# A feed-forward's second chunk: its last two blocks go up by seven products, the biases reach x by DMA, and the last chunk is reordered

## The chip, the cores and the metric

One Trainium2 chip, one of its cores. The metric is the device time of one execution in microseconds (us); of several runs the median is given. A core has five engines that matter here, each with its own queue, worked off in order: TensorE (PE; its weight loads are shown as PEld), VectorE (DVE), ScalarE (ACT), GpSimd (POOL, here almost only a queue that issues DMAs) and SyncE (SP, which issues the loads of weights).

## The reference, cut to what matters

Two layers run over 512 frames of width 1024. Each layer has two feed-forwards (hidden width 2816), and around every part stands a normalisation:

```
def swiglu_ffn(x, w_gu, w_d):
    g, u = jnp.split(x @ w_gu, 2, axis=-1)
    return (jax.nn.silu(g) * u) @ w_d

for i in range(DEPTH):                                    # DEPTH = 2
    x = layer_norm(DN_ALPHA * x + 0.5 * swiglu_ffn(x, ffn1_wgu[i], ffn1_wd[i]), ...)
    mix = mlstm_mixer(x, ...) if i == 0 else gmlp_mixer(x, ...)
    x = layer_norm(DN_ALPHA * x + mix, ...)
    x = layer_norm(DN_ALPHA * x + 0.5 * swiglu_ffn(x, ffn2_wgu[i], ffn2_wd[i]), ...)
    x = layer_norm(DN_ALPHA * x + sigmoid(x @ ple_wg[i] + ple_bg[i]) * (p[i] @ ple_wp[i]), ...)
```

So there are four feed-forwards. `layer_norm` ends with a gain and a bias over the width. The arithmetic is float32.

## The kernel before

**Numbers in two parts.** TensorE reads a rounded form of float32. So every operand is held as a high part (`whi`, `fhi`, `xh`) and a low part, the rest (`wlo`, `flo`, `xl`), and each product is three matmuls (`mm3`, lines 388 to 390): high by high, high by low, low by high. ACT makes a weight's high part by a copy (L275). The low part is either a subtraction on DVE (L284 at once; L290 when it was put off) or, for some weights, a second ACT pass that writes the negative of the high part (L281), onto which a DMA that POOL issues adds the source (L282).

**A feed-forward** (`ffn`) runs over the 2816 hidden columns in chunks of 2, 4, 4, 4, 4 and 4 blocks of 128 (`FFN_CHUNKS`). While a chunk goes up (x times the gate and up weights), the chunk before it goes down in seven products of a Strassen-like scheme (`Group`, PSUM tiles `gps`). Each down product needs a form of the hidden activations (`form`: `fhi`, `flo`) and a form of the down weights (`forms`, tiles `wquarter`), and its result is added to the residual x in SBUF (`xt`) by two DVE instructions (`residual`, L761 or L763).

- In chunks 0 and 1 (`c < UP_FROM`) the way up is plain: one tile of gate columns, then one of up columns, 24 matmuls of 512 columns each (`sup`, `fps`). After an even tile ACT takes the sigmoid-weighted gate, after an odd one DVE multiplies it in (L1192), and a down product follows.
- From chunk 2 on, two blocks go up together by seven products instead of eight (`up_products`, `UpPair`, PSUM tiles `ups`), each of 24 matmuls of 256 columns. Here s counts the products of a chunk; s modulo 7 is the product's kind r. After every odd s a down product follows. The weights come as four quarters of 512 KB (tiles `wbox`); the forms for r = 2 and r = 4 are made in place by two DVE instructions each (`up_forms`, functions `s2`, L140 and L141, and `s3`, L148 and L149). `UP_BY_DMA` and `UP_BY_DMA_2` list the kinds whose low part goes by DMA, in a chunk's first and second pair.
- The seven products need sums and differences of quarters of x (`UpForms`: t1 to t4). They are made in ten steps, one after a tile, while chunks 0 and 1 go up; the rest of t3 and t4 follows in the first products of chunk 2.

**The normalisation's gain and bias** of three feed-forwards' inputs (all but the first) are put off: x itself gets them later (`Norm.finish`, L755 and L756, one DVE instruction each for a quarter of the frames, tile `gb`), from `run_affine` at the end of chunk 0 and in chunk 1.

**The order** of the instructions is the order in which the code issues them; each engine works off its own part of it and waits at semaphores. `Weights.fill` runs ahead: whenever a product gives its weight tile back (four `main` tiles, two for the down weights), it splits the next weights in one fixed list (`W.order`), the loads of which SP issues as buffers come free.

Of the kernel before, what the change touches and what calls it, by code (L numbers as in the profile page):

```python
# [11 lines left out]
F32R = mybir.dt.float32r  # L12
AF = mybir.ActivationFunctionType
OP = mybir.AluOpType
# [3 lines left out]
P = 128  # L18
# [26 lines left out]
PLE_EXTRA = 3  # L45
UP_BY_DMA = (1, 3, 4, 5, 6)
UP_BY_DMA_2 = (1, 3, 5, 6)


class Weights:  # L50
# [4 lines left out]
    def __init__(self, nc, raw_pool, split_pool):  # L55
        self.nc = nc
        self.pools, self.free = {"main": split_pool}, {"main": W_BUFS, "none": 0}
        self.raw_pools, self.raw_bufs = {"raw": raw_pool}, {"raw": RAW_BUFS}
        self.raw_free, self.raw_at, self.raw_tags = deque(range(RAW_BUFS)), {}, {}
        self.loads, self.left, self.raws = [], [], {}  # L60
        self.queues, self.held_raws = defaultdict(deque), defaultdict(deque)
        self.order, self.next_split, self.in_place, self.by_dma = [], 0, set(), set()
        self.ready, self.taken, self.held = deque(), deque(), []
        self.apart, self.pending, self.made, self.after, self.formed = False, deque(), {}, {}, set()
        self.boxes, self.rank, self.loaded_at, self.clock = [], {}, {}, 0

    def open(self, kind, pool, n):
        self.pools[kind], self.free[kind] = pool, n
# [177 lines left out]

    def fill(self, most=1000, low=None, meanwhile=None):

        while most and self.next_split < len(self.order):
# [108 lines left out]
def hybrid_trunk(ctx: ExitStack, tc, x, p, ln_g, ln_b, ffn1_wgu, ffn1_wd, ffn2_wgu, ffn2_wd,  # L358
# [110 lines left out]

    FFN_CHUNKS = [2, 4, 4, 4, 4, 4]  # L470
    LAST = len(FFN_CHUNKS) - 1
    UP_FROM = 2
    turn_p = []

    def ffn_weights(wgu, wd, name, ple=False):
        starts = [sum(FFN_CHUNKS[:c]) for c in range(LAST + 1)]

        def forms(c):
            m = FFN_CHUNKS[c] // 2

            def quarter(i, j):
                k = starts[c] + m * i
                return kp(wd)[:, k:k + m, j * 512:(j + 1) * 512]
            loads = [W.add_load(quarter(i, j), n, name) for i, j, n in ((0, 0, 2), (0, 1, 1), (1, 1, 1), (1, 0, 2))]
            return W.forms("rows", *((j, slice(None)) for j in loads))

        first = len(W.order)
        for at in range(starts[UP_FROM]):
            if at == 0 or at == starts[UP_FROM] - 1:
                W.add(*((kp(wgu)[:, :, c0:c0 + P], [slice(None)]) for c0 in (at * P, HID + at * P)))  # L490
            elif at % 2:
                add_pairs(wgu, at * P, HID + at * P)
        tiles = W.order[first:]
        del W.order[first:]
        for c, n in enumerate(FFN_CHUNKS):
            down_w = deque(forms(c - 1) if c else ())
            if c >= UP_FROM:
                products = []
                for b in range(starts[c], starts[c] + n, 2):
                    products += W.up_forms(*(W.add_load(kp(wgu)[:, k:k + 4, c0:c0 + 2 * P], 1, "box")  # L500
                                             for c0 in (b * P, HID + b * P) for k in (0, 4)),
                                            by_dma=UP_BY_DMA if b == starts[c] else UP_BY_DMA_2)
                for s, product in enumerate(products):
                    W.order.append(product)
                    if s % 2:
                        W.order.append(down_w.popleft())
                continue
            for i in range(2 * n):
                W.order.append(tiles[2 * starts[c] + i])
                if down_w:  # L510
                    W.order.append(down_w.popleft())
        if ple:
            W.add_hook("rows", lambda hi, lo: turn_p.pop()(hi, lo))
        add_rows(wd, starts[LAST], 4, ["rowsx", "rows", "main", "main"] if ple else ["main", "rows", "rowsx", "rows"])


    ML_SLOTS = (2, 3, 4, 5, 6, 7, 11)
# [191 lines left out]
    class Norm:  # L709
# [41 lines left out]
            self.prepare(t)  # L751
            self.scale(t)

        def finish(self, t):
            vec.tensor_mul(xt[:, t], xt[:, t], self.g_bc)  # L755
            vec.tensor_add(xt[:, t], xt[:, t], self.b_bc)  # L756

    def residual(t, half, ps, first):
        dst = xt[:, t, half * 512:(half + 1) * 512]
# [9 lines left out]
        if hooks:  # L769
            hooks.pop(0)()  # L770

    def run_affine(n=1):
        for _ in range(n):
            if affine:
                affine.pop(0)()

    def set_hooks(norm):
        def turn(t, half):
            return lambda: turn_x(t, halves=(half,), norm=norm)

        def last_turn():
            turn(TB - 1, 1)()
            W.refill(4)

        hooks.extend([turn(TB - 2, 0), turn(TB - 2, 1), turn(TB - 1, 0), last_turn])
        if norm.deferred:
            affine.extend([lambda t=t: norm.finish(t) for t in range(TB)])

    def down(hs, first, norm=None, lazy=False, defer=False):

# [195 lines left out]
    class UpForms:  # L986


        def __init__(self, pool, late):
# [4 lines left out]
            both = act.tile([P, 2, 4, 256], F32R, name="t1", tag="gb")  # L994
            self.t1, self.t2, self.t4 = [both[:, 0], both[:, 1]], [], []
            self.t3 = self.quarter(0, 1)
            whole, halves = slice(0, 4), (slice(0, 2), slice(2, 4))

# [17 lines left out]
                    vec.tensor_sub(a[i], a[i], c[:, s])  # L1016

            def split_t1():
                for i, s in enumerate(halves):
# [89 lines left out]
    def ffn(layer, k, rows, late, prepare=None):  # L1109
        with stage_pool("forms", 2) as fpool, stage_pool("quarters", Q_BUFS) as qpool, \  # L1110
# [14 lines left out]

            group, hs, norm, formed = None, [], None, None

            def up_products(c, n, h):
                nonlocal norm
                for s in range(7 * n // 2):  # L1130
                    b, r = s // 7 * 2, s % 7
# [18 lines left out]
                    if s % 2:  # L1150
# [3 lines left out]
                    if s == 12 and h is not None:  # L1154
# [11 lines left out]
            for c, n in enumerate(FFN_CHUNKS):  # L1166
                if c < LAST:
                    h = hpool.tile([P, 4, SEQ], F32, name="h", tag="h")[:, :n]
                elif prepare is not None:
                    prepare()  # L1170
                if c == UP_FROM - 2:
                    formed = UpForms(tpool, late)
                W.apart = c >= UP_FROM
                if c >= UP_FROM:
                    next_group = up_products(c, n, h if c < LAST else None)
                    if c < LAST:
                        next_group.form()
                    group.add()
                    group = next_group
                for i in range(2 * n if c < UP_FROM else 0):  # L1180
                    b = i // 2
                    ps = project()
                    W.clock += 2
                    if group is not None and i:
# [3 lines left out]
                        sca.activation(sg, ps, AF.Silu)  # L1188
                        W.release()
                    else:  # L1190
                        hf = h[:, b] if c < LAST else tmp_tile("hf")
                        vec.scalar_tensor_tensor(hf, sg, 0.5, ps, op0=OP.mult, op1=OP.mult)  # L1192
                        if c == LAST:
                            hs.append(halves(W.spare(name)))
                            split(*hs[b], hf)
                        W.release()
                        run_hook()
                    if group is not None and i < 7:
                        group.product()
                        W.release(kind="rows")  # L1200
                        group.form()
                    if c == 1 and i < 3:
                        run_affine()
                    if formed is not None and (i and c == UP_FROM - 2 or i > 0 and c == UP_FROM - 1):
                        formed.step()
                    if c and i == 6:
                        next_group = Group(h, fpool)
                        next_group.form()
                if c < UP_FROM and c:
                    group = next_group  # L1210
                    group.form()
                if c == UP_FROM - 1:
                    while formed.steps:
                        formed.step()
                if c == 0:
                    group = Group(h, fpool, c == 0)
                    group.form()
                    group.form()
                if c == 0:
                    run_affine()  # L1220
            W.apart = False
            return down(hs, False, norm, lazy=layer == 0, defer=prepare is not None)

    def ffn_stage(layer, k):
# [725 lines left out]
```

## Time and profile before

| | |
|---|---|
| median of 3 runs | 2196.67 us (2195.52 to 2196.89) |
| the profiled execution, its own time | 2193.39 us |
| its span, first to last instruction | 2191.7 us |
| PE busy | 2170.3 us of the span (99%), 12821 matmuls |
| DVE busy | 1760.5 us (80%) |
| ACT busy | 1208.1 us (55%) |
| POOL busy | 226.3 us (10%) |
| mean granted TensorE clock | 0.999 |

The profiled execution is 3.3 us below the median. Busy time of matmuls is longer than their pace, since they are pipelined: one with 512 columns is shown with 0.39 us and follows the one before it by 0.23 us. So PE is judged by starts and by the idle time ahead of an instruction, not by its busy share.

### The profile page before, as it was taken

To read this page: it belongs to the slowest core of one execution; us is meant where nothing else is said; L and a number is where in the kernel's file an instruction comes from. 1 tells how busy PE (TensorE), PEld (TensorE's weight loads), DVE (VectorE), ACT (ScalarE), POOL (GpSimd) and SP (SyncE) were. 2 spreads that over 40 slices of the span, in tenths; PEclk is the share of its full clock that TensorE was granted. 3 is DMA by queue.
4 is the path that set the end of the run, shared out by engine and by line. 5 is a ranking of instruction groups with operands and counts; after the bars stand their busy time and mean duration, and the time that the engine had idled before them with its cause. 6 is when DMAs were issued, how large, how long until landed. Compare 5 with 4: busy or idle time off the path is not lost.

```text
span 2191.7 us, 32537 instructions
## 1 busy us (share of the span) xinstructions
PE 2170.3 (99%) x12821; PEld 1922.0 (88%) x12821; DVE 1760.5 (80%) x2532; ACT 1208.1 (55%) x1668; POOL 226.3 (10%) x279
## 2 busy tenths in 40 slices
PE   9999999999999999999999999999999999999998
PEld 8899997888888889999888899997888888999987
DVE  5898877786767789888887998877788679988887
ACT  4576656454546445667444566655345553666642
POOL 1011100011101101111000011110001100111100
PEclk9999999999999999999999999999999999999999
DMA  6587764366857426887531587754437743777651
GB/s 187 156 204 184 172 153 136 92 154 128 155 130 154 135 81 163 200 194 172 173 125 58 153 207 186 176 145 135 144 77 140 168 135 116 179 191 179 135 183 58
DMA packets 228097, 329.46 MB, mean 150 GB/s; under 512 B 9140, under 2 KB 163892, under 8 KB 227944
## 3 DMA queue, kind: packets, MB, share of 16 engines
q1 hardware_dynamic: 169104, 211.83, 29.8%
q0 software_dynamic: 52224, 100.86, 27.5%
q10 hardware_dynamic: 6616, 14.69, 1.9%
q8 instruction: 101, 1.65, 0.3%
q14 instruction: 52, 0.43, 0.1%
HBM read 224.58 MB, written 2.11 MB: 103 GB/s over the span
## 4 chain that ended last, share of the span: by engine, by line
PE 78%; DVE 11%; issue 4%; ACT 4%; DMA 3%; SPq 0%; POOL 0%; DVEq 0%; ACTq 0%; POOLq 0%
PE ups L390 7%; PE ups L388 7%; PE ups L389 7%; PE gps L388 6%; PE gps L389 6%; PE gps L390 6%; DMA wlo<-wbox 2%; PE dps L389 2%; PE dps L390 2%; PE dps L388 2%; DVE wlo L290 2%; PE fps L388 2%; PE fps L389 1%; PE fps L390 1%; ACT whi L275 1%
## 5 line engine op out<-in xcount | busy, mean ns | idle before, releaser
L275 ACT ACTIVATE whi<-wbox 128x1024 fp32r<-128x1024 f32 x224 | 235.7, 1054 | 242.2 <-DVE wbox L141 96.9
L390 PE MATMUL ups<-xh,wlo 128*128 128x256 f32 x1024 | 290.3, 284 | 3.2 <-DMA wlo<-wbox 3.2
L388 PE MATMUL ups<-xh,whi 128*128 128x256 f32 x1024 | 289.9, 283 | 0.0
L389 PE MATMUL ups<-xl,whi 128*128 128x256 f32 x1024 | 289.7, 283 | 0.0
L275 ACT ACTIVATE whi<-wraw 128x1024 fp32r<-128x1024 f32 (+1 forms) x212 | 217.3, 1046 | 96.7 <-DVE wraw L119 22.6
L388 PE MATMUL gps<-whi,fhi 128*128 128x512 f32 x644 | 253.0, 393 | 0.4
L389 PE MATMUL gps<-wlo,fhi 128*128 128x512 f32 x644 | 252.2, 392 | 0.0
L390 PE MATMUL gps<-whi,flo 128*128 128x512 f32 x644 | 251.4, 390 | 0.0
L282 POOL DMA_DIRECT2D wlo<-wbox x144 | 122.2, 848 | 1076.8 <-ACT wlo L281 705.0
L763 DVE TENSOR_TENSOR xt<-xt,gps 128x512 f32<-128x512 f32 x302 | 194.9, 680 | 26.7 <-PE gps L390 26.7
L284 DVE TENSOR_TENSOR wlo<-wraw,whi 128x1024 fp32r<-128x1024 f32 (+1 forms) x140 | 167.6, 1214 | 41.8 <-ACT whi L275 40.9
L390 PEld LDWEIGHTS ups<-xh,wlo 128*128 128x128 f32 x1024 | 196.2, 192 | 4.3 <-DMA wlo<-wbox 4.2
L388 PEld LDWEIGHTS ups<-xh,whi 128*128 128x128 f32 x1024 | 196.1, 192 | 3.8 <-ACT us L1085 1.6
L389 PEld LDWEIGHTS ups<-xl,whi 128*128 128x128 f32 x1024 | 196.1, 192 | 2.3
L275 ACT ACTIVATE whi<-wquarter 128x1024 fp32r<-128x1024 f32 (+1 forms) x140 | 135.3, 966 | 77.0 <-DVE wquarter L119 28.9
L281 ACT ACTIVATE wlo<-wbox 128x1024 fp32r<-128x1024 f32 x144 | 150.4, 1044 | 0.0
L390 PEld LDWEIGHTS gps<-whi,flo 128*128 128x128 f32 x644 | 120.9, 188 | 26.9
L388 PEld LDWEIGHTS gps<-whi,fhi 128*128 128x128 f32 x644 | 121.3, 188 | 23.9 <-issue 1.6
L389 PEld LDWEIGHTS gps<-wlo,fhi 128*128 128x128 f32 x644 | 121.3, 188 | 21.6
L944 DVE TENSOR_TENSOR flo<-h,fhi 128x512 fp32r<-128x512 f32 (+1 forms) x140 | 88.5, 635 | 57.6 <-ACT fhi L941 57.0
L290 DVE TENSOR_TENSOR wlo<-wquarter,whi 128x1024 fp32r<-128x1024 f32 x104 | 126.6, 1218 | 0.0
L388 PE MATMUL fps<-xh,whi 128*128 128x512 f32 x288 | 112.2, 390 | 0.0
(365 smaller groups left out, 5822.4 us busy)
## 6 DMA issues: line engine op xcount, KB each, us to landing
wlo<-wbox POOLq DMA_DIRECT2D x144, 512.0 KB, 5.8
wbox<-in_ffn_wgu_dram SPq DMA_DIRECT2D x128, 512.0 KB, 4.9
wquarter<-in_ffn_wd_dram SPq DMA_DIRECT2D x64, 512.0 KB, 5.8
wraw<-in_ml_w_in_dram SPq DMA_DIRECT2D x24, 1024.0 KB, 5.8
wlo<-wraw POOLq DMA_DIRECT2D x48, 512.0 KB, 6.4
wraw<-in_ffn_wgu_dram SPq DMA_DIRECT2D x15, 1024.0 KB, 6.0
wraw<-in_gm_w_in_dram SPq DMA_DIRECT2D x15, 1024.0 KB, 5.6
wraw<-in_ffn_wgu_dram SPq DMA_DIRECT2D x17, 512.0 KB, 4.8
```

Source lines behind the costliest of these rows:

```text
L275: self.nc.scalar.activation(hi[:, s], src[:, s], AF.Copy)
L281: self.nc.scalar.activation(lo[:, s], src[:, s], AF.Copy, scale=-1.0)
L282: self.nc.gpsimd.dma_start(lo[:, s], src[:, s], accum_op=OP.add)
L284: self.nc.vector.tensor_sub(lo[:, s], src[:, s], hi[:, s].bitcast(F32))
L290: self.nc.vector.tensor_sub(lo, src, hi.bitcast(F32))
L388: mm(ps, st[0], mv[0], start=start, stop=False, skip_group_check=more)
L389: mm(ps, st[0], mv[1], start=False, stop=False, skip_group_check=more)
L390: mm(ps, st[1], mv[0], start=False, stop=stop, skip_group_check=more)
L763: vec.tensor_add(dst, dst, ps)
L944: vec.tensor_sub(lo, src, hi.bitcast(F32))
```

## The change

- `UP_FROM` gives way to `PLAIN = 4`: the first four blocks go up plainly (chunk 0 and the first two blocks of chunk 1), and the last two blocks of chunk 1 become a pair that goes up by seven products, with the down products of chunk 0 between them. This is done in all four feed-forwards.
- The steps of `UpForms` start a chunk earlier, after the first tile, and end with chunk 1's fourth tile. t2 is made last of the first eight, and its low part now goes by ACT and a DMA of POOL, not by DVE.
- Gain and bias come at four earlier places (`AFFINE_AT`), and inside a feed-forward the bias is added by a DMA that POOL issues (line 768 after), no longer by DVE.
- In the last chunk the last down product follows s = 12 instead of s = 13 (`down_after`), the second pair's form r = 5 has its low part subtracted by DVE (`UP_BY_DMA_LAST`), and the weights of the next stage are not split before the last product up (`W.limit`).

The diff, cut to its core:

```
+UP_BY_DMA_LAST = (1, 3, 6)
...
-    UP_FROM = 2
+    PLAIN = 4
+    AFFINE_AT = ((0, 1), (0, 2), (1, 0), (1, 1))
+    def plain_blocks(c):
+        return min(FFN_CHUNKS[c], max(0, PLAIN - sum(FFN_CHUNKS[:c])))
+    def down_after(c, s):
+        return s == 12 if c == LAST and s > 11 else s % 2 == 1
...
+            plain = plain_blocks(c)
+            for i in range(2 * plain):
                 W.order.append(tiles[2 * starts[c] + i])
                 if down_w:
                     W.order.append(down_w.popleft())
+            if plain < n:
+                products = []
+                for b in range(starts[c] + plain, starts[c] + n, 2):
+                    products += W.up_forms(..., by_dma=UP_BY_DMA if b == starts[c] + plain
+                                           else UP_BY_DMA_2 if c < LAST else UP_BY_DMA_LAST)
+                for s, product in enumerate(products):
+                    W.order.append(product)
+                    if down_after(c, s):
+                        W.order.append(down_w.popleft())
...
-        def finish(self, t):
+        def finish(self, t, by_dma=False):
             vec.tensor_mul(xt[:, t], xt[:, t], self.g_bc)
-            vec.tensor_add(xt[:, t], xt[:, t], self.b_bc)
+            if by_dma:
+                pool.dma_start(xt[:, t], self.b_bc, accum_op=OP.add)
+            else:
+                vec.tensor_add(xt[:, t], xt[:, t], self.b_bc)
...
             def split_t2():
-                split(f32r(self.t2, late, "whi"), f32r(self.t2, late, "wlo"), c)
+                hi, lo = f32r(self.t2, late, "whi"), f32r(self.t2, late, "wlo")
+                sca.activation(lo, c, AF.Copy, scale=-1.0)
+                nc.gpsimd.dma_start(lo, c, accum_op=OP.add)
+                sca.activation(hi, c, AF.Copy)
             self.steps = [
                 x22, lambda: joined(b, 0, 1), t3, lambda: joined(c, 0, 0), lambda: vec.tensor_add(c, b, c),
-                split_t2, t1, split_t1]
+                t1, split_t1, split_t2]
...
-            def up_products(c, n, h):
+            def up_products(c, n, h, plain):
-                for s in range(7 * n // 2):
+                for s in range(7 * (n - plain) // 2):
...
-                    if c == UP_FROM and s in formed.last:
+                    if plain and s in formed.last:
                         formed.last[s]()
...
-                    if s % 2:
+                    if down_after(c, s):
                         group.product()
...
+                if c == LAST:
+                    W.limit = ffn_ends.pop(0)
-                for i in range(2 * n if c < UP_FROM else 0):
+                for i in range(2 * plain):
...
-                    if c == 1 and i < 3:
-                        run_affine()
+                    if (c, i) in AFFINE_AT:
+                        run_affine(by_dma=True)
-                    if formed is not None and (i and c == UP_FROM - 2 or i > 0 and c == UP_FROM - 1):
+                    for _ in range(1 if (c, i) < (1, 2) else 2):
                         formed.step()
```

What this does to the queues is shown at three places. A chunk's tiles are counted from 0, gate and up tiles alike.

**DVE, where chunk 1's fourth tile is multiplied in, in the first feed-forward of layer 1** (`h<-sg,fps` is that instruction; `xt<-xt,gps` adds a down product; `x_d` and the low part `xl<-x_f` belong to t4 and t3; the two `wbox<-wbox` make the form r = 4 of the next pair). Before, the same instruction of the chunk's eighth tile, with the pair of chunk 2 behind it:

```order
L761 SCALAR_TENSOR_TENSOR xt<-xt,gps 128x512 x2
L1192 SCALAR_TENSOR_TENSOR h<-sg,fps 128x512
L284 TENSOR_TENSOR wlo<-wquarter,whi 128x1024
L1037 TENSOR_TENSOR x_d<-x_d,x_f_11495 128x512 x2
L944 TENSOR_TENSOR flo<-h,fhi 128x512
L394 TENSOR_TENSOR xl<-x_f_11494,xh 128x4x256
L148 TENSOR_TENSOR wbox<-wbox 128x1024
L149 TENSOR_TENSOR wbox<-wbox 128x1024
```

Now, behind the fourth tile:

```order
L396 TENSOR_TENSOR t_11945<-x_a,t_11945 128x512 x2
L775 SCALAR_TENSOR_TENSOR xt<-xt,gps 128x512 x2
L1206 SCALAR_TENSOR_TENSOR h<-sg,fps 128x512
L286 TENSOR_TENSOR wlo<-wquarter,whi 128x512
L958 TENSOR_TENSOR flo<-h,fhi 128x256
L1013 TENSOR_TENSOR x_d<-xh,xl 128x512 x2
L1055 TENSOR_TENSOR x_d<-x_d,x_f_11693 128x512 x2
L775 SCALAR_TENSOR_TENSOR xt<-xt,gps 128x512 x2
L396 TENSOR_TENSOR xl<-x_f_11692,xh 128x4x256
L150 TENSOR_TENSOR wbox<-wbox 128x1024
L151 TENSOR_TENSOR wbox<-wbox 128x1024
```

The pair's form r = 4 now stands behind the fourth tile and not behind the eighth, with the lows of t1 ahead of it and one more addition to `xt` between.

**ACT at the same place, now** (`whi<-wbox` and `wlo<-wbox` are high and negated high of the pair's forms, `t_11945` is t1, `t_wlo` and `t_whi` are t2, `us<-ups` takes the pair's first product out of PSUM):

```order
L277 ACTIVATE whi<-wbox 128x1024
L955 ACTIVATE fhi<-h 128x256
L395 ACTIVATE t_11945<-x_a 128x512 x2
L1039 ACTIVATE t_wlo<-x_f_11693 128x1024
L1041 ACTIVATE t_whi<-x_f_11693 128x1024
L277 ACTIVATE whi<-wbox 128x1024
L283 ACTIVATE wlo<-wbox 128x1024
L277 ACTIVATE whi<-wquarter 128x512
L955 ACTIVATE fhi<-h 128x256
L1103 ACTIVATE us<-ups 128x512
L395 ACTIVATE xh<-x_f_11692 128x4x256
L277 ACTIVATE whi<-wbox 128x1024
```

t1 and t2 now stand in one piece between the forms r = 2 and r = 3 of the pair, and ahead of the sixth down form's high part (`whi<-wquarter`); before, t2 came two tiles earlier than t1.

**DVE at the end of a feed-forward** (the first of layer 0; `wlo<-wraw` are lows of the last down weights and, behind them, of the next stage; `wquarter<-us` are lows of the last hidden activations). Before:

```order
L1088 TENSOR_TENSOR us<-us,ups 128x512
L290 TENSOR_TENSOR wlo<-wraw,whi 128x1024 x2
L1104 SCALAR_TENSOR_TENSOR us<-us 128x512
L394 TENSOR_TENSOR wquarter<-us,wquarter 128x2x256
L1104 SCALAR_TENSOR_TENSOR us<-us,ups 128x512
L394 TENSOR_TENSOR wquarter<-us,wquarter 128x2x256
L763 TENSOR_TENSOR xt<-xt,gps 128x512 x2
L290 TENSOR_TENSOR wlo<-wraw,whi 128x1024 x3
```

Now:

```order
L1106 TENSOR_TENSOR us<-us,ups 128x512
L292 TENSOR_TENSOR wlo<-wraw,whi 128x1024 x2
L777 TENSOR_TENSOR xt<-xt,gps 128x512 x2
L1122 SCALAR_TENSOR_TENSOR us<-us 128x512
L396 TENSOR_TENSOR wquarter<-us,wquarter 128x2x256
L1122 SCALAR_TENSOR_TENSOR us<-us,ups 128x512
L396 TENSOR_TENSOR wquarter<-us,wquarter 128x2x256
L292 TENSOR_TENSOR wlo<-wraw,whi 128x1024
L286 TENSOR_TENSOR wlo<-wraw,whi 128x1024 x3
```

The last addition of a down product to `xt` moved ahead of the last activations, and three lows of the next stage stand behind the last low of the down weights.

More of the change, by code (lines that the diff above doesn't have):

```diff
@@ L1153, in up_products @@
                         group.form(True)
-                    if s == 12 and h is not None:
+                    if s == steps - 2 and h is not None:
                         next_group = Group(h, fpool)
@@ L1170, in ffn @@
                     prepare()
-                if c == UP_FROM - 2:
+                plain = plain_blocks(c)
+                if c == 0:
                     formed = UpForms(tpool, late)
[L1173 to L1179, printed above, removed]
-                for i in range(2 * n if c < UP_FROM else 0):
-                    b = i // 2
+                W.apart = not plain
+                if c == LAST:
+                    W.limit = ffn_ends.pop(0)
+                for i in range(2 * plain):
                     ps = project()
@@ L1190, in ffn @@
                     else:
[L1191 to L1195, printed above, removed]
+                        vec.scalar_tensor_tensor(h[:, i // 2], sg, 0.5, ps, op0=OP.mult, op1=OP.mult)
                         W.release()
                         run_hook()
-                    if group is not None and i < 7:
+                    if group is not None:
                         group.product()
```

63 lines of the change are left out of this document (28 added, 35 removed).

## The prediction

> **What bounds the kernel now.** First the page's head and its groups, then who waited on PE. In a group's line stand busy us, mean ns of one, idle time before it and who ended it; in a line of waits the us in total, how often, and the longest.
>
> ```profile
> span 2191.7 us, 32537 instructions
> PE 2170.3 (99%) x12821; PEld 1922.0 (88%) x12821; DVE 1760.5 (80%) x2532; ACT 1208.1 (55%) x1668; POOL 226.3 (10%) x279
> L756 DVE TENSOR_TENSOR xt<-xt,gb 128x1024 f32<-128x1024 f32 x20 | 24.5, 1225 | 0.7
> PE dps L389 <- DVE wlo L290: 4.8, 4, 1.6
> PE ups L390 <- DMA wlo<-wbox: 3.9, 6, 1.0
> ```
>
> PE never rests: its waits inside the feed-forwards add up to 4.8 + 3.9 = 8.7 us. So a change gains only by giving PE less to do or by ending these waits, and it loses wherever PE begins to wait. What PE's work costs shows in four stretches of the first feed-forward of layer 1: plain tiles, a pair of products, a down product of chunk 2, and chunk 1 from its fifth tile to its end (columns: us, then busy us and number for PE, PEld, DVE, ACT, POOL, then clock, DMA share, GB/s).
>
> ```profile
> 1182.60:1193.30 10.70, 10.70 (x49) 8.85 (x48) 8.74 (x13) 2.27 (x4) 0.00 (x0) 1.00 0.35 106
> 1267.20:1272.80 5.60, 5.60 (x49) 5.60 (x48) 5.57 (x6) 0.83 (x1) 0.84 (x1) 1.00 0.95 208
> 1264.50:1267.10 2.60, 2.60 (x13) 2.15 (x12) 2.57 (x5) 2.54 (x4) 0.00 (x0) 1.00 0.89 234
> 1215.20:1241.40 26.20, 26.05 (x115) 21.29 (x114) 24.37 (x33) 12.75 (x18) 0.88 (x1) 1.00 0.64 198
> ```
>
> A matmul of 512 columns takes about 0.227 us (48 in 10.9), one of 256 about 0.120 us (48 in 5.75). DVE is nearly as full as PE: 24.4 us of 26.2 in the stretch that is replaced.
>
> **PE's part of the change.** Per feed-forward four plain tiles go, 96 x 0.227 = 21.8 us, and seven products come, 168 x 0.120 = 20.1 us. PE is spared 1.65 us four times, 6.6 us in all, if it never waits. Down products keep their number.
>
> **DVE's part.** Out per feed-forward: four lows of plain tiles (1.14 each), two L1192 (0.60), t2's low (1.14), and in three of the four feed-forwards four bias additions (1.23). In: four subtractions for the pair's forms, two late lows, five takes out of PSUM. The sum falls by some 6 us where the biases go and hardly changes in the first, but the work must now be done earlier: t1 to t4 serve PE four tiles sooner. So it is the place that counts, and there I follow DVE row by row. PE's anchors, and DVE in chunk 1 (start, us, what):
>
> ```profile
> 1215.18 0.39 PE L388 MATMUL fps<-xh,whi 128*128 128x512 f32 x1
> 1241.45 0.28 PE L388 MATMUL ups<-xh,whi 128*128 128x256 f32 x1
> ...
> 1195.70 0.69 DVE L284 TENSOR_TENSOR wlo<-wquarter,whi 128x512 fp32r<-128x512 f32 x1 [1.23 <-ACT whi L275]
> ...
> 1208.34 1.22 DVE L755 TENSOR_TENSOR xt<-xt,gb 128x1024 f32<-128x1024 f32 x1
> 1209.60 1.23 DVE L756 TENSOR_TENSOR xt<-xt,gb 128x1024 f32<-128x1024 f32 x1
> 1210.74 1.22 DVE L1000 TENSOR_TENSOR x_f<-xh,xl 128x1024 f32<-128x1024 f32 x1
> 1211.87 1.28 DVE L763 TENSOR_TENSOR xt<-xt,gps 128x512 f32<-128x512 f32 x2
> 1220.10 1.27 DVE L761 SCALAR_TENSOR_TENSOR xt<-xt,gps 128x512 f32<-128x512 f32 x2
> 1221.30 0.68 DVE L1192 SCALAR_TENSOR_TENSOR h<-sg,fps 128x512 f32<-128x512 f32 x1
> 1221.90 0.68 DVE L284 TENSOR_TENSOR wlo<-wquarter,whi 128x512 fp32r<-128x512 f32 x1
> 1239.70 1.22 DVE L284 TENSOR_TENSOR wlo<-wbox,whi 128x1024 fp32r<-128x1024 f32 x1 [1.19 <-ACT whi L275]
> ```
>
> The L1192 at 1221.30 is that of the fourth tile. Its matmuls and the down product behind them (1.36 us) had ended at 1215.18: DVE is 7.5 us late here already before the change. It recovers while the plain tiles 5 to 8 pass. Exactly these are taken away. By starts that follow each other, a DVE instruction of 512 elements steps on by 0.60 us, one of 1024 by 1.14, one that must wait for the one before by 1.25.
>
> When does DVE reach this instruction now? From the down form at 1195.7, which PE sets in both kernels, it is spared three bias additions (3.75), one gain and one `x_f` that moved ahead (1.25, 1.14), and gets t1's two subtractions and two lows (2.4), the two subtractions of form r = 2 (2.4) and the wait for that form's high part (1.19, as in the last line above). That is 0.15 less: 1221.2, as late as before.
>
> Behind it now stand, up to the end of the pair's form r = 4: itself 0.60, a down low 0.60, `flo` 0.42, `x_d` twice two (2.4), an addition to `xt` (1.2), t3's low (1.14), two subtractions (2.4), together 8.8 us. Besides, the down low waits for its high part: ACT makes t1, t2 and form r = 3 first, 2 x 0.5 + 4 x 0.95 + 0.6 = 5.4 us, against 3.5 us of DVE work since the same point, so 1.9 us (bounds 0, if ACT runs ahead, and 4). DVE ends form r = 4 at 1221.2 + 8.8 + 1.9 = 1231.9. From there to PE it is a chain that chunk 2 shows:
>
> ```profile
> 1249.81 1.23 DVE L149 TENSOR_TENSOR wbox<-wbox 128x1024 f32<-128x1024 f32 x1
> 1251.07 1.06 ACT L275 ACTIVATE whi<-wbox 128x1024 fp32r<-128x1024 f32 x1 [4.38 <-DVE wbox L149]
> 1252.04 1.04 ACT L281 ACTIVATE wlo<-wbox 128x1024 fp32r<-128x1024 f32 x1
> 1253.37 0.85 POOL L282 DMA_DIRECT2D wlo<-wbox  x1 [8.74 <-ACT wlo L281]
> DMA to landing us min/median/max: 4.5/4.5/4.5
> ...
> wlo<-wbox POOLq DMA_DIRECT2D x144, 512.0 KB, 5.8
> 310.85 8.45 DMA wlo<-wbox
> ```
>
> High, negated high, issue and landing (4.5 for this very one): 1253.37 + 4.5 - 1251.04 = 6.8 us. I take it, since it is the same form in the same place of a pair; all such DMAs have a median of 5.8, one took 8.45. So the low part of r = 4 is there at 1238.7. PE could start that product at 1215.18 + 4 x 2.87 + 2 x 1.36 = 1229.4 (four products, two down products of 6 matmuls) and needs the low 0.24 later. **PE is held for 9.1 us**, part of it already at the third product: t2's low leaves ACT at about 1220.5, so its DMA lands at 1225.3 against 1222.4 (at 1222.4 plus the wait of the down product for its addition on DVE). That wait costs nothing of its own, the later one swallows it; some 6.4 us remain for PE in one piece ahead of r = 4.
>
> Chunk 1 then ends at 1238.7 - 0.24 + 3 x 2.87 + 1.36, plus 0.6 for the lows of r = 5 and 6 that follow by DMA at 3 us distance: 1249.0 against 1241.45 before, **+7.6 us**. The two other feed-forwards with a put-off gain have the same order, so 3 x 7.6 = 22.8.
>
> The first feed-forward has no gain and bias to shed:
>
> ```profile
> 62.39 0.68 DVE L1192 SCALAR_TENSOR_TENSOR h<-sg,fps 128x512 f32<-128x512 f32 x1
> 60.72 0.39 PE L388 MATMUL gps<-whi,fhi 128*128 128x512 f32 x1
> 87.92 0.28 PE L388 MATMUL ups<-xh,whi 128*128 128x256 f32 x1
> ```
>
> DVE is only 1.7 us late there, but gets 4.8 + 1.2 of new work and waits, less 1.14 (`x_f`) and about 0.95 of a wait now filled: 66.3. Plus 8.8 and 2 is 77.1, the low at 83.9, the chunk's end at 94.2 against 87.92, **+6.3**.
>
> **PE's clock.** Nowhere before does PE rest for 2 us, except at the end:
>
> ```profile
> 2182.95 0.28 PE L390 MATMUL gps<-whi,xl 128*128 128x256 f32 x1
> 2182.00:2186.00 4.00, 1.23 (x11) 1.03 (x9) 3.31 (x11) 0.42 (x1) 0.00 (x0) 0.93 0.00 0
> 2186.00:2190.00 4.00, 0.00 (x0) 0.00 (x0) 2.65 (x5) 0.00 (x0) 0.92 (x1) 0.50 0.28 109
> ...
> 1.43 3.36 PE L1903 MATMUL warm<-ident 128*128 128x128 f32 x16 [1.43 <-POOL ident masks.py:199]
> 7.20 1.26 PE L1903 MATMUL warm<-ident 128*128 128x128 f32 x10
> ```
>
> The granted clock halves about 2.2 us after the last matmul (0.93 over four us is 0.56 us at a half), and at the start 16 transposes take 0.21 us each that later take 0.126: 1.3 us lost. A wait of 6.4 us is longer than 2.2, so I add 1.3 four times, 5.2 us (bounds 0 and 2.6 each). The Trainium skill, "TensorE: Matmul & The Clock Gate", Part 1, has the rule: after an idle window of about 3.4 us the array's clock falls to half and needs a busy window of that length to come back. The trace agrees as far as it shows this; by the page a restart costs an estimated 1.7 us, and the sum would be 1.6 higher.
>
> **The end of a feed-forward.** Two rows of DVE from the last chunk of the first one:
>
> ```profile
> 314.95 0.69 DVE L944 TENSOR_TENSOR flo<-h,fhi 128x512 fp32r<-128x512 f32 x1 [2.10 <-ACT fhi L941]
> ...
> 322.29 0.69 DVE L1088 TENSOR_TENSOR us<-us,ups 128x512 f32<-128x512 f32 x1 [1.81 <-PE ups L390]
> ```
>
> Form r = 5 of the last pair no longer waits for a DMA, its box comes free for the last down weights some us earlier, and the last down low is no longer behind the last addition. On the other side DVE gets one late low (1.22), which lies in its idle time there (2.10 and 1.81 us ahead of two instructions), and three lows of the next stage, hidden by the 12.7 us of the matmuls down. I take all 8.7 us of PE's waits as gone, those at chunk 2's end too; bounds 0 and 8.7.
>
> **Other costs.** The bias DMAs: three issues ahead of the pair's first low, the fourth between two of them, 0.85 us of POOL each; the first two land by about 1195, their `xt` is next used at 1202; the fourth lands about 1215.5, three us before ACT may write t1 over its source. Nothing, covered by DVE's own lateness; without that cover ACT would wait. SP's loads: the boxes' buffers come free with the sixth and seventh tile's split (1183 to 1188), they land by 1195, needed at 1206 and 1212. Nothing.
>
> **The sum.** 22.8 + 6.3 + 5.2 - 8.7 = +25.6 us; PE's 6.6 are inside the chunk ends. Against the median of 2196.67 that is 2222 (against the profiled execution's own 2193.39, which is 3.3 below that median, 2219).
>
> The Trainium skill, "DMA: Bandwidth & Descriptors", Anatomy of one DMA, gives a fit for DMAs that POOL issues, 2.0 us plus the bytes by 436 per ns: an estimated 3.2 us for 512 KB, and the sum would be about 5 us lower. The trace has 4.5 at the least and 5.8 in the middle, so the measurement decides.
>
> **The rivals.**
> - *DVE keeps up (the other side).* If form r = 4 ended on DVE by 1229.6 - 6.8 = 1222.8, 9 us sooner than I reckon, PE would not wait: -6.6 - 8.7, some 2181. It breaks even where the hold is about 3.8 us per feed-forward instead of 9. For it: DVE's sum falls by 6 us. Against it: the row at 1221.30, which the change hardly moves. 0.13.
> - *Half a hold*, 4 to 5 us: ACT and DVE interleave better and no wait of 1.9 arises, the clock stays up; 2195 to 2200. 0.07.
> - *The DMAs crowd.* More of them at the same place (t2, r = 3, 4, 5, 6 within 15 us): landings of 8 instead of 4.5 us, as the one at 310.85: 4 x 3.5 more, 2236. 0.12.
> - *The end gains nothing*: the waits there only find another cause, 2231. 0.10.
> - My forecast, 0.58; its own range 2208 to 2230.
>
> Slower by over 0.2% (4.4 us, about what a measurement here can tell) in 0.58 + 0.12 + 0.10 = 0.80, within it 0.07, faster 0.13. The range 2196 to 2236 leaves out the case in which DVE keeps up and the far ends.
>
> **What would show it.** PE should wait in `ups` L390 for a DMA `wlo<-wbox` four times for 5 to 7 us, near 40 us after the feed-forward's staged tiles end, with `ups` L389 at `t_wlo` waiting some 2 us before; the granted clock should dip there. DVE should have no idle time from the first tile on until then. PE's waits at `dps` L389 should be gone. I am wrong if DVE reaches the fourth tile's multiplication some 5 us earlier than it does now, or if PE's waits in chunk 1 stay under 4 us.

## The result, and the profile after

The changed kernel takes 2228.11 us (median of five runs, 2227.16 to 2231.84), the kernel before 2196.67: a ratio of 1.0154 (95% interval 1.0143 to 1.0165), 31.4 us slower; 2222 was predicted. The profiled execution of the changed kernel is its slowest run (2231.84 us) and that of the kernel before lies 3.3 us under its median, so the two traces differ by more than the medians: 2230.1 - 2191.7 = 38.4 us. Everything below that is split by place is a part of these 38.4. (The mean granted clock is 0.989 in the profiled execution and 0.991 to 0.992 in the other four, so some of the difference to the median is clock.)

The page's head and its list of waits of PE (us in total, how often, the longest):

```profile
span 2230.1 us, 33273 instructions
PE 2178.2 (98%) x13109; PEld 1944.7 (87%) x13109; DVE 1765.0 (79%) x2540; ACT 1244.1 (56%) x1712; POOL 254.3 (11%) x311
PE ups L390 <- ACT us L1103: 30.4, 8, 6.3
PE dps L391 <- DVE wlo L292: 6.0, 2, 3.0
PE gps L390 <- DVE xt L775: 3.1, 3, 1.1
PE ups L391 <- DMA t_wlo<-x_f: 1.1, 4, 0.3
```

Two waits in each feed-forward are new, eight in all, ahead of products r = 2 and r = 4. But they are put down to ACT's line 1103, which takes a product out of PSUM, not to a DMA as predicted. Where the time went shows when each feed-forward is cut at PE's anchors: the first matmul behind the staged tiles (a feed-forward's first three, PSUM tiles `sup`), the first of chunk 2, the first down, and the end of the 54 matmuls down that follow. The anchors of the first feed-forward of layer 1, before (chunk 2 starts at 1241.45 there) and after:

```profile
1182.51 0.40 PE L388 MATMUL fps<-xh,whi 128*128 128x512 f32 x1
```

```profile
1197.67 0.40 PE L390 MATMUL fps<-xh,whi 128*128 128x512 f32 x1
...
1267.87 0.28 PE L390 MATMUL ups<-xh,whi 128*128 128x256 f32 x1
```

Chunks 0 and 1 take 70.20 us instead of 58.94. The four feed-forwards (us, before to after):

| feed-forward | to chunk 2 | chunks 2 to 5 | 54 matmuls down |
|---|---|---|---|
| layer 0, first | 59.12 to 68.45 | 239.79 to 237.73 | 14.28 to 12.27 |
| layer 0, second | 58.89 to 69.31 | 241.27 to 238.69 | 13.54 to 17.20 |
| layer 1, first | 58.94 to 70.20 | 238.99 to 237.73 | 14.00 to 12.27 |
| layer 1, second | 58.93 to 70.17 | 239.90 to 238.61 | 13.54 to 18.30 |
| sum of differences | +42.2 | -7.2 | +4.7 |

The rest of the program is 1.3 us shorter. The loss is in chunk 1, and there it is decided in one place, ahead of product r = 4. DVE first, then ACT, POOL and PE (start, us, what; in brackets the idle time before and who ended it), first feed-forward of layer 1:

```profile
1210.86 0.69 DVE L286 TENSOR_TENSOR wlo<-wquarter,whi 128x512 fp32r<-128x512 f32 x1 [2.32 <-ACT whi L277]
1237.67 0.68 DVE L1206 SCALAR_TENSOR_TENSOR h<-sg,fps 128x512 f32<-128x512 f32 x1
1240.10 0.69 DVE L286 TENSOR_TENSOR wlo<-wquarter,whi 128x512 fp32r<-128x512 f32 x1 [1.74 <-ACT whi L277]
1247.03 1.23 DVE L151 TENSOR_TENSOR wbox<-wbox 128x1024 f32<-128x1024 f32 x1
```

```profile
1248.29 1.06 ACT L277 ACTIVATE whi<-wbox 128x1024 fp32r<-128x1024 f32 x1 [6.49 <-DVE wbox L151]
1249.25 1.04 ACT L283 ACTIVATE wlo<-wbox 128x1024 fp32r<-128x1024 f32 x1
1250.20 1.13 ACT L1060 ACTIVATE t_f<-x_d 128x512 fp32r<-128x512 f32 x2
1251.24 1.04 ACT L277 ACTIVATE whi<-wbox 128x1024 fp32r<-128x1024 f32 x1
1252.18 1.04 ACT L283 ACTIVATE wlo<-wbox 128x1024 fp32r<-128x1024 f32 x1
1253.13 0.61 ACT L1117 ACTIVATE us<-us 128x512 f32<-128x512 f32 x1
1253.65 0.61 ACT L277 ACTIVATE whi<-wquarter 128x512 fp32r<-128x512 f32 x1
1254.17 0.40 ACT L955 ACTIVATE fhi<-h 128x256 fp32r<-128x256 f32 x1
1254.48 0.57 ACT L1103 ACTIVATE us<-ups 128x512 f32<-128x512 f32 x1
```

```profile
1250.59 0.84 POOL L284 DMA_DIRECT2D wlo<-wbox  x1 [9.89 <-ACT wlo L283]
DMA to landing us min/median/max: 4.5/4.5/4.5
1255.10 0.58 PE L390 MATMUL ups<-xh,whi 128*128 128x256 f32 x1 [6.35 <-ACT us L1103]
```

DVE had caught up with PE at 1210.86. It ends form r = 4 at 1248.26; ACT has stood idle for 6.5 us in front of it. From there two chains run to PE. One is the predicted one: high, negated high, DMA, landing at 1250.59 + 4.49 = 1255.08. The other is ACT's own queue: product r = 4 adds to the PSUM bank that r = 2 wrote, so ACT must have taken r = 2 out, and that instruction stands behind nine others and ends at 1255.05. PE goes on at 1255.10. The two gates open 0.03 us apart (0.03 to 0.10 in the other feed-forwards); the profile can't say which of them holds PE.

The second loss is the clock. Granted clock is the third column from the right:

```profile
1248.70:1250.90 2.20, 0.05 (x1) 0.00 (x0) 1.35 (x3) 2.20 (x4) 0.31 (x1) 1.00 0.06 17
1250.90:1261.20 10.30, 6.10 (x28) 6.10 (x29) 3.93 (x7) 8.21 (x12) 2.23 (x3) 0.50 0.93 189
1261.20:1264.00 2.80, 2.80 (x24) 2.76 (x23) 2.77 (x4) 2.22 (x3) 0.85 (x1) 1.00 0.96 232
```

It is halved 2.2 us into the wait and stays so for 10.2 us (1250.93 to 1261.17; the row takes in a little more), 6.1 of them with PE at work. At the half clock matmuls of 256 columns follow each other by 0.213 us instead of 0.120, those of 512 by 0.427 instead of 0.227: less than twice as far apart. So the 28 matmuls of this stretch lose 2.6 us. Ahead of the program's end there are seven such stretches in the trace, 44.4 us in all, 34.1 of them with PE busy. In them lie 115 matmuls of 256 columns in chunk 1, which lose 10.7 us, and 22 of 512 in the down stages, which lose 4.4: 15.1 us.

In the down stages the second feed-forward of each layer has a wait of 3.0 us where there were 0.9 before (ACT and PE, layer 0):

```profile
1088.98 2.95 ACT L277 ACTIVATE whi<-wraw 128x1024 fp32r<-128x1024 f32 x3 [1.45 <-PE gps L392]
1091.84 0.62 ACT L395 ACTIVATE wquarter<-us 128x512 fp32r<-128x512 f32 x1
...
1096.36 0.50 PE L391 MATMUL dps<-wlo,wquarter 128*128 128x512 f32 x1 [2.98 <-DVE wlo L292]
```

The last down product, now ahead of the last product up, frees weight tiles earlier; ACT fills three of them at once, and only then makes the high part of the last activations, for which DVE waits with the low of a down weight behind it.

### The profile page after: what moved, and what is told of

It is laid out like the page before. It is cut to its first block, busy times and chain, and to the rows that moved or that the text cites. A ratio compares the mean times of both kernels' runs of the same rounds, so it can differ in the third digit from the quotient of the medians.

```text
span 2230.1 us, 33273 instructions
## 1 busy us (share of the span) xinstructions
PE 2178.2 (98%) x13109; PEld 1944.7 (87%) x13109; DVE 1765.0 (79%) x2540; ACT 1244.1 (56%) x1712; POOL 254.3 (11%) x311
## 5 line engine op out<-in xcount | busy, mean ns | idle before, releaser
L277 ACT ACTIVATE whi<-wbox 128x1024 fp32r<-128x1024 f32 x252 | 265.2, 1054 | 281.5 <-DVE wbox L143 117.6
L390 PE MATMUL ups<-xh,whi 128*128 128x256 f32 x1152 | 330.8, 287 | 23.5 <-ACT us L1103 23.5
L392 PE MATMUL ups<-xh,wlo 128*128 128x256 f32 x1152 | 330.4, 287 | 0.0
L391 PE MATMUL ups<-xl,whi 128*128 128x256 f32 x1152 | 330.3, 287 | 0.0
L390 PEld LDWEIGHTS ups<-xh,whi 128*128 128x128 f32 x1152 | 225.5, 196 | 27.6 <-ACT us L1103 25.2
L391 PEld LDWEIGHTS ups<-xl,whi 128*128 128x128 f32 x1152 | 225.3, 196 | 2.4
L392 PEld LDWEIGHTS ups<-xh,wlo 128*128 128x128 f32 x1152 | 225.3, 196 | 0.0
L283 ACT ACTIVATE wlo<-wbox 128x1024 fp32r<-128x1024 f32 x160 | 167.1, 1044 | 0.0
L292 DVE TENSOR_TENSOR wlo<-wquarter,whi 128x1024 fp32r<-128x1024 f32 (+1 forms) x116 | 139.2, 1200 | 0.0
L955 ACT ACTIVATE fhi<-h 128x512 fp32r<-128x512 f32 (+1 forms) x140 | 80.3, 574 | 40.5 <-DVE h L1206 23.4
```

Source lines behind the costliest of these rows:

```text
L277: self.nc.scalar.activation(hi[:, s], src[:, s], AF.Copy)
L283: self.nc.scalar.activation(lo[:, s], src[:, s], AF.Copy, scale=-1.0)
L292: self.nc.vector.tensor_sub(lo, src, hi.bitcast(F32))
L390: mm(ps, st[0], mv[0], start=start, stop=False, skip_group_check=more)
L391: mm(ps, st[0], mv[1], start=False, stop=False, skip_group_check=more)
L392: mm(ps, st[1], mv[0], start=False, stop=stop, skip_group_check=more)
```

## The experiments

Theory A is the prediction's: PE is held by the low part of r = 4, which comes late by DMA. Theory B: PE is held by ACT's eviction of r = 2, stuck in ACT's queue. Both start from DVE's late form. Medians are of four or more runs, beside runs of the kernel before on the same chip; all edits are to the changed kernel unless said otherwise, and are shown cut to their core.

**The two halves of the change.** `end_only` is the kernel before with the new end of a feed-forward; `no_end` is the changed kernel with the old end:

```
-        return s == 12 if c == LAST and s > 11 else s % 2 == 1
+        return s % 2 == 1
...
-UP_BY_DMA_LAST = (1, 3, 6)
+UP_BY_DMA_LAST = UP_BY_DMA_2
...
-                if c == LAST:
-                    W.limit = ffn_ends.pop(0)
```

> The kernel before, with the change at the end of a feed-forward alone (last down product after s = 12, form r = 5 of the last pair subtracted by DVE, no weights of the next stage before the last product up). The prediction's step (all of PE's 8.7 us of waits there go): 2197 - 8.7 = 2188. What the trace of the changed kernel shows by stages instead: chunks 2 to 5 shorter by 2.1, 2.6, 1.3 and 1.3 us, the down stage by 2.0 and 1.7 us in the first feed-forward of each layer, but longer by 3.7 and 4.8 in the second of each, where PE waits 3.0 us for a low of the down weights: together -2.5, so 2194.

> The changed kernel with the old end of a feed-forward: only chunk 1 and the biases are changed. By stages of the trace chunk 1 costs 42 us (9.3, 10.4, 11.3, 11.2); so with the old end about 2228 + 2.5 = 2231 by the trace, and 2228 + 8.7 = 2237 by the prediction's step. Below 2225 the end would itself be a large part of the loss.

`end_only` 2190.89 against 2195.01 (0.9983, interval 0.9974 to 0.9992), `no_end` 2232.42 (1.0165, 1.0148 to 1.0182). So the end gains about 4 us by itself, between the two figures expected of it, and chunk 1 with its biases costs 37. In `end_only`, too, PE has the new wait in the second feed-forwards:

```profile
PE dps L391 <- DVE wlo L292: 6.0, 2, 3.0
```

**Which gate holds PE.** `r4_dve` takes the DMA out of the chain. `r45_dve_evict` also puts ACT's eviction of r = 2 ahead of its copies for r = 5, whose low part goes to DVE too (`W.release` is what lets ACT split the next weights):

```
-  by_dma=UP_BY_DMA if b == starts[c] + plain else ...
+  by_dma=(UP_BY_DMA_2 if plain else UP_BY_DMA) if b == starts[c] + plain else ...
# r45_dve_evict: UP_BY_DMA_LAST there, and
-                    W.release()
+                    if not plain or s != 1:
+                        W.release(2 if plain and s == 2 else 1)
```

> The changed kernel, but the low part of form r = 4 of chunk 1's pair is subtracted by DVE, not by ACT and a DMA. Theory A (the prediction's): PE waits for that low, which lands 6.8 us after DVE made the form. DVE would have it some 5 us sooner, so PE is held about 2 us instead of 6 and its clock stays up: (4 to 5 + about 2.7 of clock) x 4 = 27 to 30 us less, 2198 to 2202. Theory B: PE waits for ACT, which takes product r = 2 out of the PSUM bank that r = 4 adds to; this eviction stands in ACT's queue behind the copies of forms r = 4 and r = 5, and the DMA lands at the same moment only by chance (trace: eviction over at 1255.05, landing at 1255.08, PE on at 1255.10). Then only ACT's one copy (0.95 us) is saved: 4 us less, 2224.

> As r4_dve, and ACT takes product r = 2 out of PSUM ahead of its copies of form r = 5 (the split of r = 5 is put off from s = 1 to s = 2, its low is DVE's too). Theory A: nothing beyond r4_dve, 2198 to 2202. Theory B: the eviction ends at about 1251.7 instead of 1255.05 on the trace's clock, so PE is held 3 us less, four times, and its clock drops less or not at all (0 to 2.7 each): 13 to 24 us less than 2228, 2204 to 2215, and the wait that is left is still ahead of r = 4, on ACT.

`r4_dve` 2223.49 (1.0130, 1.0115 to 1.0145), `r45_dve_evict` 2213.71 (1.0087, 1.0072 to 1.0102): theory B both times. In `r4_dve` the low part of r = 4 (DVE), the eviction (ACT) and PE, first feed-forward of layer 1:

```profile
1246.16 1.23 DVE L292 TENSOR_TENSOR wlo<-wbox,whi 128x1024 fp32r<-128x1024 f32 x1 [0.53 <-ACT whi L277]
1250.31 0.57 ACT L1103 ACTIVATE us<-ups 128x512 f32<-128x512 f32 x1
1250.93 0.38 PE L390 MATMUL ups<-xh,whi 128*128 128x256 f32 x1 [4.16 <-ACT us L1103]
```

The low is there at 1247.39 and PE still waits until 1250.93, 0.05 us after the eviction. With the eviction moved ahead PE follows it again (`r45_dve_evict`):

```profile
1242.77 0.57 ACT L1103 ACTIVATE us<-ups 128x512 f32<-128x512 f32 x1
1243.40 0.58 PE L390 MATMUL ups<-xh,whi 128*128 128x256 f32 x1 [2.99 <-ACT us L1103]
```

No run takes the eviction away and leaves the DMA, so what the DMA would hold by itself is known only from the times above.

**Is DVE's lateness the root of both?** Three runs: t2 ahead of t1 (`t2_early`), work taken from ahead of form r = 4 (`dve_early`), work added ahead of it (`bias_dve`):

```
-                t1, split_t1, split_t2]                      # t2_early
+                split_t2, t1, split_t1]
-    AFFINE_AT = ((0, 1), (0, 2), (1, 0), (1, 1))             # dve_early
+    AFFINE_AT = ((0, 0), (0, 1), (0, 2), (0, 3))
-            self.steps += [x21, t4]
+            self.tail = [x21, t4]                            # run behind s == 1
-            self.last = {..., 1: t4_high, 2: t4_low}
+            self.last = {..., 2: t4_high, 3: t4_low}
-                        run_affine(by_dma=True)              # bias_dve
+                        run_affine()
```

> The changed kernel with t2 made and split one tile earlier, ahead of t1 and not behind it. Theory B (ACT's queue holds PE): t2's two copies (1.9 us) no longer stand ahead of form r = 3's; ACT takes product r = 0 out of PSUM 1.9 us sooner, so PE's 2.0 us ahead of r = 2 nearly go; DVE's wait of 1.74 us for a down weight's high part goes too, so form r = 4 and all behind it come 1.7 us sooner: 4 x 1.7 = 7 us less, 2221. If it is only DVE's amount of work that counts, form r = 4 comes no sooner: 2228, and r = 4 waits longer by what r = 2 waits less.

> The changed kernel with DVE work taken from ahead of the pair's form r = 4: the gains at (0,0) to (0,3) instead of (0,1) to (1,1) (two of 1.14 us less ahead of it, in three feed-forwards), and t4's four additions (2.4 us) behind it. Nothing is left out. If DVE's lateness is the root (theory A and B agree on that): 4 x 2.4 + 3 x 2.3 = 16.5 us, plus 4 x 1.0 since t4's ACT copies no longer stand ahead of the eviction, plus some clock: 2200 to 2208. If ACT's own copies set the time whatever DVE does: 4 x 1.0 alone, 2224.

> The changed kernel with the biases added by DVE again, at the same places. If DVE's lateness is the root: the two additions behind the last place where DVE had caught up (1.14 to 1.25 us each) make form r = 4 later by 2.3 us in three feed-forwards: 7 us more, 2235. If the bias DMAs crowd out other transfers (one of them landed after 9.1 us): no loss or a gain, 2222 to 2229.

| | median | ratio to before | form r = 4 done, us after the staged tiles | chunk 2 starts |
|---|---|---|---|---|
| changed kernel | 2228.11 | 1.0154 | 50.6 | 70.2 |
| `t2_early` | 2223.84 | 1.0133 (1.0116 to 1.0150) | 49.0 | 67.7 |
| `dve_early` | 2215.15 | 1.0090 (1.0075 to 1.0105) | 46.6 | 65.0 |
| `bias_dve` | 2238.99 | 1.0200 (1.0185 to 1.0215) | 54.1 | 72.3 |

The last two columns are of the first feed-forward of layer 1. The order is the one expected if DVE is the root. Form r = 4 comes earlier by nearly what was reckoned (-1.6 for 1.7, -4.0 for 4.7) and later by half again as much (+3.5 for 2.3). The two gains are at most about 60% of those expected, the loss is half again as large. The interval of `t2_early` just overlaps that of the changed kernel, so its gain is sure only in its trace; 2215 for `dve_early` lies between the two figures expected of it, nearer the one for DVE. In `dve_early` waits stay ahead of r = 2 and of r = 4, and the clock halves behind the first one, short as it is (the last section says when it does):

```profile
1232.63 0.39 PE L390 MATMUL ups<-t_whi,whi 128*128 128x256 f32 x1 [1.40 <-ACT us L1103]
1243.40 0.39 PE L390 MATMUL ups<-xh,whi 128*128 128x256 f32 x1 [1.40 <-ACT us L1103]
1244.78 0.58 PE L392 MATMUL ups<-xh,wlo 128*128 128x256 f32 x1 [0.88 <-DMA wlo<-wbox]
```

```profile
1234.10:1237.60 3.50, 3.50 (x19) 3.50 (x18) 3.47 (x4) 0.00 (x0) 0.00 (x0) 0.51 0.47 89
```

Product r = 4 waits 1.40 us for the eviction and then 0.88 for the DMA's landing: once ACT is early enough, the predicted gate is the next one.

**All at once, and the next wait.** `all4` joins `r45_dve_evict`, `t2_early` and `dve_early`; in `all5` t4's additions and split come one product later still (`s == 2`, `3: t4_high, 4: t4_low`):

> All of r45_dve_evict (r = 4 and r = 5 low by DVE, eviction ahead of r = 5's copies), t2_early and dve_early at once. If they add: 2228 - 14.4 - 7 - 20 = 2187; chunk 1 can give back 33 us at most over r45_dve_evict (its ends lie 6.5, 8.6, 9.9 and 8.3 us behind unhindered products), so not under 2181. If another wait comes up behind them (the lows of r = 5 and 6, the down weights' lows): 2195 to 2208.

> As all4, with t4's additions one product later (behind s = 2, its split at s = 3 and 4). In all4 the hold of 3.6 us had moved from r = 4 to r = 5: t4's additions stood on DVE, and so its copies and those of r = 5 on ACT, ahead of the eviction of r = 3. If that is the cause, r = 5 is held 0.9 us at most and the clock stays up: (2.7 + 2.7) x 4 = 21 us less than all4's 2213, 2191 (2188 to 2197). If the queues are simply too full, the wait goes on to r = 6: over 2203.

`all4` 2212.92 (1.0079, 1.0064 to 1.0094), no better than `r45_dve_evict` and above both figures expected: the parts don't add. DVE, ACT and PE in `all4`, first feed-forward of layer 1:

```profile
1236.71 1.29 DVE L1013 TENSOR_TENSOR x_d<-xh,xl 128x512 f32<-128x512 f32 x2
1237.92 1.28 DVE L1055 TENSOR_TENSOR x_d<-x_d,x_f 128x512 f32<-128x512 f32 x2
```

```profile
1238.70 1.17 ACT L1060 ACTIVATE t_f<-x_d 128x512 fp32r<-128x512 f32 x2 [1.85 <-DVE x_d L1055]
...
1243.13 0.57 ACT L1103 ACTIVATE us<-ups 128x512 f32<-128x512 f32 x1
```

```profile
1243.76 0.39 PE L390 MATMUL ups<-xh,whi 128*128 128x256 f32 x1 [3.62 <-ACT us L1103]
```

Now r = 5 waits, for the eviction of r = 3: ACT waits for t4's additions on DVE and then has 4.4 us of copies, t4's own among them, ahead of that eviction (1238.70 to 1243.13). The same trap one product on, set by my own edit. `all5` takes it away: 2199.69 (1.0021, 1.0012 to 1.0030), 13 us less than `all4`, though not the 21 expected; chunk 2 starts 60.7 us after the staged tiles (60.6 in the first feed-forward of layer 0).

**Versions to beat both.** `best2` is `all5` with the new end only in the first feed-forward of each layer, `end_first` the kernel before with that end there; `best3` moves the rest of `UpForms`' steps one tile forward:

```
-                    for _ in range(1 if (c, i) < (1, 2) else 2):
+                    for _ in range(2 if (c, i) == (0, 3) else 1):
                         formed.step()
```

> As all5, with the new end in the first feed-forward of each layer alone and the old one in the second, where the new one makes PE wait 3.0 us for a down weight's low. By stages (from chunk 2 to the end of the 54 matmuls down) the old end was 2.2 and 4.3 us shorter there: 2191 - 6.5 = 2185, faster than the kernel before (2196) and than end_first.

> The kernel before with the new end in the first feed-forward of each layer alone. In end_only the second ones were 1.3 us longer than before each: 2190.9 - 2.5 = 2188.4. Were the 3.0 us of wait and the clock behind it all the difference there, 2180.

> As best2, with the rest of UpForms' steps one tile earlier (t2's addition behind chunk 0's fourth tile, its split behind chunk 1's first, t1 behind the second). In best2 chunk 2 still starts 1.7 us later than in the kernel before, with 2.2 us of waits in five small pieces, four of them behind DVE's form r = 4 or its additions. If DVE's place in the order is the root, 2.3 us of its work move ahead of the point where it has caught up, the waits ahead of r = 4 (0.6 and 0.7) and of the down product (0.6) go, each with some 0.2 us of refilling the array: 4 x 2 = 8 us less, 2187. If what is left is ACT's and the DMAs' doing: 2193 to 2195.

`best2` 2194.88 (0.9996, 0.9987 to 1.0005), missed by 10: its base, `all5`, came out 9 above its own forecast. `end_first` 2189.13 (0.9970, 0.9959 to 0.9982). `best3` 2187.88 (0.9965, 0.9951 to 0.9978), as forecast. What PE still waits for in `best3`:

```profile
PE gps L392 <- DVE flo L958: 3.8, 3, 1.3
PE xps L642 <- DVE xt L751: 3.1, 2, 1.8
PE ups L392 <- DVE wlo L292: 2.3, 4, 0.7
PE dps L391 <- DVE wlo L292: 1.8, 2, 0.9
```

`best3` beats the kernel before and the changed one, but its interval overlaps that of `end_first`: with the long holds ahead of r = 2 and r = 4 gone, the seven products of chunk 1 are still worth nothing that these runs can tell. Its chunk 2 starts at 58.1 us in the first feed-forward (59.1 before) and at 59.4 in the others (58.9 before).

## Why the prediction was right, and where not

- **PE spared 6.6 us; the replaced plain tiles were DVE's time to recover.** The 6.6 were never seen: even in `best3` chunk 2 starts 1.0 us earlier in one feed-forward and 0.5 later in three. The second half is right: `bias_dve` and `dve_early` move the time with DVE's lateness, and the fourth tile's multiplication comes 40.0 us after the staged tiles, 38.7 reckoned (1221.2 - 1182.51).
- **DVE's path to form r = 4 (8.8 + 1.9 us).** Right within 0.2: 1248.26 - 1237.67 = 10.59, with the wait for ACT 1.74 instead of 1.9.
- **The DMA's chain of 6.8 us holds PE.** The length is right (1248.26 to 1255.08), the conclusion is the step that failed. ACT's queue, with the eviction of r = 2 behind form r = 4, ends at the same moment, and without the DMA PE is still held 4.2 us instead of 6.35 (`r4_dve`, layer 1's first). I had followed what r = 4 needs from the weights' side and not what it needs of its PSUM bank. The wait of some 2 us ahead of r = 2 came as well, but it, too, is ACT's: 1.97 us for the eviction of r = 0 (0.99 in the very first feed-forward), and only 0.2 to 0.3 for t2's low by DMA.
- **Chunk 1's end, 22.8 + 6.3 = 29.1 us without the clock.** Measured 42.2 - 10.7 = 31.5. That it comes so close is luck: the gate that I had left out opens at the same moment as the one that I followed.
- **The clock, 5.2 us.** Mis-sized: 15.1. I took 1.3 us per hold from the program's start; the clock stays at a half for 3.4, 6.8 or 10.2 us, short waits bring it down too, and 4.4 of the 15.1 lie in the down stages, where I had reckoned with no wait.
- **The end, all 8.7 us gone.** Most of it came: chunks 2 to 5 are 7.2 us shorter (more than their waits of 3.9; what else went there was not looked into) and two of the down stages 3.7. In the other two the wait grew to 3.0 us, which I did not see: I asked what is freed for DVE and not what ACT does with tiles that come free earlier. All four together gain 6.9 without the clock behind that wait, 2.5 with it, and 4 in `end_only`.
- **Biases by DMA cost nothing.** Right, and more: DVE would have cost 11 us (`bias_dve`).
- The sum: 31.5 + 15.1 - 6.9 - 1.3 = 38.4 between the traces; predicted were 25.6, and between the medians it is 31.4. The clock is the term that differs most, by 9.9.
- Of the rivals, "DVE keeps up" and "the DMAs crowd" didn't come: the low of r = 4 landed after 4.49 to 4.56 us in all four feed-forwards. Nor did "half a hold": PE's waits in chunk 1 add up to 7.6 to 9.6 us in each feed-forward, where 9.1 were reckoned for layer 1's first. "The end gains nothing" came in part: 2.5 of the 8.7 us are left.

## What to carry to other kernels

A form that one engine makes late stops another engine's queue at its first reader, and everything behind that reader is late as well, evictions of PSUM banks among them; so for each product list all that it needs (weights, moving operand, bank) and follow each one's queue back. When two gates open at the same moment, the profile names one of them; only taking each away alone tells which holds. Taking work off a PE that never rests is worth only what its feeders can spare: here the replaced tiles were where DVE caught up.

## What the runs showed of the hardware

The granted clock, when it falls, is at a half for 3.41 us or a multiple of it (3.41, 6.82 and 10.24 in the changed kernel). These stretches begin on a fixed grid: in each of the 14 traces their starts lie whole multiples of 3.413 us apart, to within 0.002 (in the changed kernel 827.68, then 841.33, which is 4 steps on, 1097.33, 75 steps, and 1250.93, 45 steps).

So what counts is not how long a wait is, but how much of it falls into one window of the grid. The busy time is the profile's, with its modelled ends of matmuls. Of the 8927 windows at the full clock, all 51 with PE idle for 1.93 us or more were followed by a half clock, and none with 1.60 or less; of the 23 between these, five were. At the half clock PE must do more to get out: the full clock came back behind every window with at most 0.49 us of idle time, and behind none with 0.76 or more (82 windows). In `end_only` the two waits of 2.98 us fall differently on the grid, and only the first halves the clock (PE's busy us come first in a row):

```profile
1075.65:1079.06 3.41, 0.63 (x3) 0.19 (x1) 2.71 (x4) 2.27 (x3) 0.00 (x0) 1.00 0.02 10
1079.06:1082.47 3.41, 3.21 (x8) 2.56 (x9) 3.41 (x4) 0.36 (x1) 0.00 (x0) 0.50 0.56 180
2099.65:2103.06 3.41, 1.58 (x7) 1.32 (x8) 3.41 (x4) 1.81 (x2) 0.00 (x0) 1.00 0.15 16
2103.06:2106.47 3.41, 3.41 (x17) 2.81 (x16) 3.41 (x4) 0.00 (x0) 0.00 (x0) 1.00 1.02 378
```

In the same way a wait of 1.40 us followed by one of 0.25 brought the clock down in `dve_early`, where both fall into one window (1230.74 to 1234.16, 1.65 us idle), and a like pair in the second feed-forward of layer 1, which a border of the grid cuts in two, did not; waits of up to 1.6 us in the kernel before never did. The Trainium skill, "TensorE: Matmul & The Clock Gate", Part 1, tells of a free-running window of about 3.4 us, which the trace's multiples agree with; that a whole idle window is needed, as it has for the fall, these rows do not bear out. Why windows with 1.6 to 1.9 us of idle time go both ways is open.
